# Both score maps of differential attention on the two row halves of TensorE, the minimum written to SBUF, five banks in turn

## The chip, the core and the metric

The kernel runs on one core of a Trainium2 chip. The metric is the device time of one execution in microseconds (us). A lower time is better. Engines are named as in the profile: PE (TensorE matmuls), PEld (TensorE weight loads), DVE (VectorE), ACT (ScalarE), POOL (GpSimd) and SP (SyncE, which issues the DMAs).

## What is computed

Two layers of a decoder trunk over 1024 tokens of width 1024 in float32. Layer 0 has stick-breaking and forgetting heads, layer 1 has 8 differential heads, and each layer ends in a SwiGLU block. The change touches layer 1 alone:

```python
def differential_attention(q1, q2, k1, k2, v, lam, rel_bias):
    ...
    def block(start, end):                       # 128 queries over the causal prefix
        bias = table[t5_bucket(...)].transpose(2, 0, 1)[None]
        s1 = jnp.einsum('bhqd,bhkd->bhqk', q1[:, :, start:end], k1[:, :, :end]) * scale + bias
        s2 = jnp.einsum('bhqd,bhkd->bhqk', q2[:, :, start:end], k2[:, :, :end]) * scale + bias
        p1 = jax.nn.softmax(jnp.where(causal, s1, -jnp.inf), axis=-1)
        p2 = jax.nn.softmax(jnp.where(causal, s2, -jnp.inf), axis=-1)
        return jnp.einsum('bhqk,bhkd->bhqd', p1 - lam * p2, v[:, :, :end])
```

`q1`, `q2`, `k1`, `k2` have 64 channels each, and `v` has 128. The bias differs from a constant only within the nearest 256 keys.

## The kernel before

**Numbers.** Matmuls take float32r operands. A float32 value x is split into h (x rounded to float32r) and l = x - h, and a product is made of the three terms hh, hl and lh. So a dense projection issues three matmuls of 512 columns for each 128-channel step (`mm3`, lines 375 to 377); the value projection issues three of 256 columns (lines 466 to 468).

**Layer 1's mixer.** `mixer(1, ...)` runs eight windows, one for a head. A window (`window_odd`) makes the score rows of its head in two groups g of four 128-query rows (`g_rows`, `row_C`), mixed with the value products of the group before (`g_pv`: the weight rows are transposed by PE at line 677, split, and multiplied with V at line 691). Between these steps `paced` feeds pieces of the "filler": the projections of later heads and, at the end, most of the output projection. Each step yields its estimated PE time, and the filler is advanced in proportion to the yields' sum over a fixed window cost (18000). The build then orders the instructions of each engine by what is ready by its own estimate, so the order on PE is not that of the code.

**Scores of a row.** One projection gives both maps of a head: channels 0 to 63 of the partitions belong to map 1, channels 64 to 127 to map 2. `stack_k` and `stack_q` copy, by DMAs on SP's queue, h and l of one map on top of each other (64 + 64 partitions), so that one matmul over all 128 rows of the array gives two of the four possible terms. `scores` (line 569) then issues two matmuls for each piece of a row and each map, all four terms. A row of n = 128(i+1) keys is cut into pieces of at most 512 columns (`cuts`): over the eight rows of a head that is five pieces of 512, three of 384 and four of 256 columns. So a head has 12 pieces x 2 maps x 2 = 48 score matmuls, and the layer has 384.

**Softmax of a row.** `map_C` adds the bias to the scores in their PSUM bank, in place, and takes the running minimum (of the negated, scaled values) with `tensor_tensor_reduce` on DVE (line 623); then ACT takes the exponential out of PSUM, piece by piece (line 110), with a sum for each piece, and DVE adds the two sums of a row with two pieces (line 630). `row_C` joins the maps: two reciprocals, a product with -lambda (lines 642 to 644), a scaling of map 2 on POOL (line 645) and a multiply-add on DVE (line 646).

**Banks.** PSUM has eight banks: `rD` (two) serves projections, `rS` (three) scores, `rT` (two) transposes and norms, `rO` (one) the value product. Each set is used in turn.

Of the kernel before, what the change touches and what calls it, by code (L numbers as in the profile page):

```python
# [14 lines left out]
AF = mybir.ActivationFunctionType  # L15
# [3 lines left out]
P = 128  # L19
# [3 lines left out]
TH = 512  # L23
# [17 lines left out]
def r32(ap):  # L41
    return ap.bitcast(F32R)
# [74 lines left out]
class Trunk:  # L117
# [277 lines left out]
    def stack_k(self, src, th, KK):  # L395
# [9 lines left out]
            dma(KK[e][o, sl], t[p, 512:1024])  # L405
        self.sr.put(t)

    def head_norm(self, x, gcol, table):

        nc = self.nc  # L410
        sq, h, l = self.hf.get(), self.hr.get(), self.hr.get()
        self.S.activation(r32(h[:]), x[:], AF.Square)
        self.S.activation(sq[:], x[:], AF.Square)
        nc.vector.tensor_tensor(r32(l[:]), sq[:], h[:], ALU.subtract)
        ms = self.rT.get()
        nc.tensor.matmul(ms[:], r32(self.blk[:]), r32(h[:]), start=True, stop=False)
        nc.tensor.matmul(ms[:], r32(self.blk[:]), r32(l[:]), start=False, stop=True)
        self.hr.put(h, l)
        self.rstd(ms[:], sq[:], table)
        nc.vector.scalar_tensor_tensor(x[:], x[:], self.gains[:, gcol:gcol + 1], sq[:], ALU.mult, ALU.mult)  # L420
        self.hf.put(sq)

    def qk_half(self, which, th, w, stk, gcol, table=False, ps=None):

        ps = self.rD.get() if ps is None else ps
        self.dense_half(w[2], w[3], th, ps[:])
        src = self.hf.get()
        self.nc.vector.tensor_tensor(src[:], ps[:], self.rt[:, th * TH:th * TH + TH], ALU.mult)
        if gcol is not None:
            self.head_norm(src, gcol, table)  # L430
        if which == 0:
            if th == 0:
                stk.append([self.sr.get(), self.sr.get()])
            self.stack_k(src, th, stk[0])
        else:
            stk.append([self.sr.get(), self.sr.get()])
            self.pq = gcol is not None
            self.stack_q(src, stk[-1])
        self.hf.put(src)
        self.w_ahead(self.keep)  # L440

    def g_qk(self, st, gains=(None, None), table=False):

        stk = []
        for which in range(2):
            w = self.w_next()
            for th in range(2):
                self.qk_half(which, th, w, stk, gains[which], table)
                if th == 1:
                    self.sr.put(w[0], w[1])  # L450
                    if which == 1:
                        st.append(list(zip(*stk)))
                yield HALF

    def v_weights(self, forget):
# [42 lines left out]
    def first_project(self, st, vs, gains, accs, load, table):  # L498

        w, vh, vl = self.v_weights(False)  # L500
        wq = [self.w_next(), self.w_next()]
        V = [self.sf.get(), self.sf.get()]
        stk = []
        for th in range(2):
            load(th)
            for k in range(KC):
                for t in range(4):
                    self.v_piece(4 * th + t, k, vh, vl, self.bank[t], 256)
            self.rms(accs[th], th, True, table)
# [8 lines left out]
        st.append(list(zip(*stk)))  # L518

    def log_forget(self):  # L520

# [33 lines left out]
    def row_of(self, rows, i):  # L555
        s, o = self.ROWPOS[i]
        return rows[s][:, o:o + (i + 1) * P]

    def scores(self, i, KK, *Q):

        nc = self.nc
        n = (i + 1) * P
        cuts = [(0, max(n, 256))] if n <= 512 else ([(0, 384), (384, 640)] if n == 640 else [(0, 512), (512, n)])
        res = []
        for lo, hi in cuts:
# [44 lines left out]
    def map_C(self, i, stk, w, nb, st):  # L610

        nc = self.nc
        n = (i + 1) * P
        pcs = self.scores(i, *stk)
        near = max(n - 256, 0)
        parts = [(b, lo, min(hi, near), self.zero[:].to_broadcast([P, min(hi, near) - lo])) for b, lo, hi in pcs
                 if min(hi, near) > lo]
        b, lo, hi = pcs[-1]
        parts.append((b, lo, n, nb[:, 256 - (n - near):256]))
        m = self.pinit[:]  # L620
        for j, (b, lo, hi, add) in enumerate(parts):
            d = b[:, max(near - lo, 0) if j == len(parts) - 1 else 0:hi - lo]
            nc.vector.tensor_tensor_reduce(out=d, in0=d, in1=add, scale=-0.125, scalar=m, op0=ALU.add, op1=ALU.min,
                                           accum_out=st[:, j:j + 1])
            m = st[:, j:j + 1]
        for j, (b, lo, hi) in enumerate(pcs):
            self.S.activation(w[:, lo:hi], b[:, 0:hi - lo], AF.Exp, bias=m, scale=-1.0,
                                 accum_out=st[:, 5 + j:6 + j])
        if len(pcs) == 2:
            nc.vector.tensor_tensor(st[:, 7:8], st[:, 5:6], st[:, 6:7], ALU.add)  # L630
            return st[:, 7:8]
        return st[:, 5:6]

    def row_C(self, i, stk, rows, nb):
        nc = self.nc
        n = (i + 1) * P
        w = self.row_of(rows, i)
        p2 = self.sf.get()
        s1, s2, s3 = self.stat.get(), self.stat.get(), self.stat.get()
# [7 lines left out]
        self.sf.put(p2)  # L647

    def g_rows(self, kind, g, stk, rows, extra):
        for i in range(4 * g, 4 * g + 4):  # L650
            if kind == "A":
                self.row_A(i, stk, rows)
            elif kind == "B":
                self.row_B(i, stk, rows, *extra)
            else:
                self.row_C(i, stk, rows, *extra)
            yield max((i + 1) * P, 256) * 2 * (2 if kind == "C" else 1) / 2.4

    def g_pv(self, kind, g, rows, vv, split, done):

# [145 lines left out]
    def mixer(self, l, gains, window, window_cost, accs, load, forget=None):  # L806
# [3 lines left out]
        if l == 0:  # L810
            self.setup2()
        rows = [self.sf.get() for _ in range(4)] + [self.raw.get()]
        dense = self.filler(l, st, vs, gains, forget)
        self.dcost = 0.0
        self.o_done = 0
        V = None
        for w in range(8):
# [7 lines left out]
            att = window(w, stks, V, rows)  # L825
            self.paced(self.last(att, rows) if w == 7 else att, window_cost, dense, lo, hi)
        self.advance(dense, math.inf)

    def filler(self, l, st, vs, gains, forget):
        yield from self.project(st, vs, gains, forget)  # L830
# [40 lines left out]
    def window_odd(self, h, stks, V, rows):  # L871
# [5 lines left out]
        vv = []  # L877
        split = partial(self.split_v128, V, h % 2)
        for g in range(2):
            yield from self.stage(self.g_rows("C", g, stks, rows, (nb,)))  # L880
            fin = None
            self.sr.put(*(x[1 + g] for x in stks))
            if g == 1:
                self.sr.put(*(x[0] for x in stks))
# [8 lines left out]
    def stage(self, rows):  # L893

        pv = self.pend
        if pv is None:
            yield from rows
            return
        yield from self.mix(rows, 4, pv[0], pv[1])
        if pv[2]:  # L900
            pv[2]()

# [512 lines left out]
    def build(self):  # L1415
        nc, b = self.nc, self.bank
        self.pend = None
        self.rD, self.rS, self.rT, self.rO = Rot(b[0:2]), Rot(b[2:5]), Rot(b[5:7]), Rot(b[7:8])
        self.rF, self.rE = Rot(b[0:4]), Rot(b)
        self.make_weights()  # L1420
# [132 lines left out]
```

## Time and profile before

| | |
|---|---|
| median of three runs | 2577.13 us (2576.64 to 2579.63) |
| the profiled execution | 2576.64 us, of which 2574.9 us are its span |
| mean granted TensorE clock | 0.988 |
| busy share of the span | PE 95%, PEld 78%, DVE 76%, ACT 51%, POOL 30% |
| layer 1's mixer, first projection to first gate matmul | 1320 to 1919 us of the span |

A matmul's duration in the trace includes its way through the array, so consecutive matmuls overlap: the time one costs in a stream is the step from its start to the next one's start. "Idle before" is the time an engine had nothing running, and the name behind the arrow is what ended it. "issue" means that nothing the profile shows was waited for.

### The profile page before, as it was taken

The numbers are of one execution on the slowest core, as the hardware profiler recorded it, in microseconds if no ns is written. First come the engines' busy times: TensorE is split into PE (matmuls) and PEld (weight loads), VectorE is DVE, ScalarE is ACT, GpSimd is POOL, SyncE is SP. The second block draws the span as 40 slices with busy tenths as digits, with TensorE's granted clock in tenths as the row PEclk, the third lists the DMA queues.
The fourth block names the chain that finished last, engine by engine and source line by source line (L and its number), as shares of the span: only waits on it lengthen the run. The fifth ranks groups of instructions, "written<-read, shape, count | busy, mean of one in ns | idle before, by whom it ended". The sixth has DMA issues, their size and how long they took to land.

```text
span 2574.9 us, 34805 instructions
## 1 busy us (share of the span) xinstructions
PE 2456.4 (95%) x11896; PEld 2016.9 (78%) x11896; DVE 1946.7 (76%) x3391; ACT 1303.1 (51%) x2618; POOL 764.3 (30%) x608
## 2 busy tenths in 40 slices
PE   8898899999989999999999999998998999999999
PEld 7786778777768888888878878876777788888887
DVE  7969958987987666698576687778879866667974
ACT  5646666764732322344466576766555233234352
POOL 4112111120343322165142232223333333222910
PEclk9999999999989999999999999999999999999999
DMA  6323132465224232474333241325531422318352
GB/s 184 88 54 83 37 97 82 114 185 175 107 100 149 93 120 95 160 249 147 111 125 84 72 101 56 97 79 133 179 126 66 169 99 94 119 66 300 119 185 80
DMA packets 148270, 307.50 MB, mean 119 GB/s; under 512 B 18515, under 2 KB 24436, under 8 KB 148092
## 3 DMA queue, kind: packets, MB, share of 16 engines
q1 hardware_dynamic: 148092, 305.28, 38.0%
q8 instruction: 93, 1.52, 0.2%
q14 instruction: 85, 0.70, 0.1%
HBM read 187.74 MB, written 75.53 MB: 102 GB/s over the span
## 4 chain that ended last, share of the span: by engine, by line
PE 67%; DVE 19%; ACT 6%; issue 4%; DMA 2%; POOL 2%; SPq 0%; DVEq 0%; ACTq 0%; POOLq 0%
PE bk L1129 9%; PE bk L1130 9%; PE bk L1131 9%; PE bk L1278 5%; PE bk L1279 5%; PE bk L1280 5%; PE bk L376 4%; PE bk L375 4%; PE bk L377 4%; PE bk L691 4%; PE bk L569 3%; DVE sf L587 3%; PE bk L677 2%; DVE sr L1062 2%; ACT sf L110 2%
## 5 line engine op out<-in xcount | busy, mean ns | idle before, releaser
L102 ACT CAST sr<-sf 128x512 fp32r<-128x512 f32 (+2 forms) x536 | 337.0, 648 | 572.3 <-PE bk L1131 235.3
L1062 DVE TENSOR_TENSOR sr<-sf,sr 128x512 fp32r<-128x512 f32 x438 | 400.5, 923 | 143.9 <-ACT sr L102 142.6
L1129 PE MATMUL bk<-sr,sr 128*128 128x512 f32 x1232 | 484.3, 393 | 22.1 <-DVE hf L1153 13.3
L1131 PE MATMUL bk<-sr,sr 128*128 128x512 f32 x1232 | 482.2, 392 | 3.4 <-DVE sr L1062 3.4
L1130 PE MATMUL bk<-sr,sr 128*128 128x512 f32 x1232 | 483.0, 392 | 0.0
L375 PE MATMUL bk<-sr,sr 128*128 128x512 f32 x768 | 307.1, 400 | 6.3 <-DVE sf L989 3.5
L376 PE MATMUL bk<-sr,sr 128*128 128x512 f32 x768 | 305.5, 398 | 2.3 <-DVE sr L932 2.2
L377 PE MATMUL bk<-sr,sr 128*128 128x512 f32 x768 | 304.3, 396 | 0.0
L1129 PEld LDWEIGHTS bk<-sr,sr 128*128 128x128 f32 x1232 | 233.7, 190 | 74.1 <-DVE hf L1153 13.6
L221 POOL TENSOR_TENSOR sr<-raw,sr 128x512 fp32r<-128x512 f32 (+2 forms) x140 | 188.1, 1360 | 304.9 <-ACT sr L102 168.1
L1131 PEld LDWEIGHTS bk<-sr,sr 128*128 128x128 f32 x1232 | 233.5, 190 | 53.5 <-DVE sr L1062 4.2
L1130 PEld LDWEIGHTS bk<-sr,sr 128*128 128x128 f32 x1232 | 233.7, 190 | 47.9
L1279 PE MATMUL bk<-sr,sr 128*128 128x512 f32 x616 | 239.9, 389 | 1.4 <-DVE sr L1062 1.4
L1280 PE MATMUL bk<-sr,sr 128*128 128x512 f32 x616 | 239.6, 389 | 0.0
L1278 PE MATMUL bk<-sr,sr 128*128 128x512 f32 x616 | 239.6, 389 | 0.0
L102 ACT CAST sr<-hf 128x512 fp32r<-128x512 f32 (+1 forms) x248 | 153.8, 620 | 112.4 <-DMA hf<-td 43.5
L1062 DVE TENSOR_TENSOR sr<-hf,sr 128x512 fp32r<-128x512 f32 x178 | 180.2, 1016 | 35.7 <-ACT sr L102 34.9
L569 PE MATMUL bk<-sr,sr 128*128 128x512 f32 (+2 forms) x768 | 200.3, 359 | 7.1 <-ACT sf L110 6.3
L691 PE MATMUL bk<-hr,sr 128*128 128x512 f32 (+2 forms) x560 | 165.4, 388 | 13.9 <-DVE hr L709 11.2
L102 ACT CAST hr<-bk 128x512 fp32r<-128x512 f32 (+2 forms) x240 | 122.5, 525 | 102.8 <-PE bk L677 90.5
L375 PEld LDWEIGHTS bk<-sr,sr 128*128 128x128 f32 x768 | 145.3, 189 | 36.8 <-DVE sf L989 5.2
L709 DVE TENSOR_TENSOR hr<-bk,hr 128x512 fp32r<-128x512 f32 (+2 forms) x240 | 142.2, 603 | 39.3 <-ACT hr L102 37.5
(203 smaller groups left out, 4836.8 us busy)
## 6 DMA issues: line engine op xcount, KB each, us to landing
hf<-td SPq DMA_DIRECT2D x146, 256.0 KB, 3.1
td<-hf SPq DMA_DIRECT2D x138, 256.0 KB, 2.0
sr<-sr SPq DMA_DIRECT2D x96, 256.0 KB, 3.4
sf<-in_wg_dram SPq DMA_DIRECT2D x44, 512.0 KB, 3.3
sf<-in_wu_dram SPq DMA_DIRECT2D x44, 512.0 KB, 3.3
sf<-in_wd_dram SPq DMA_DIRECT2D x88, 256.0 KB, 4.9
raw<-in_w_dram SPq DMA_DIRECT2D x64, 256.0 KB, 2.9
sr<-sr SPq DMA_DIRECT2D x128, 128.0 KB, 2.3
```

Source lines behind the costliest of these rows:

```text
L102: self.last = self.e.copy(out, in_)
L375: nc.tensor.matmul(ps, WH[k], hH[k], start=first and k == 0, stop=False)
L376: nc.tensor.matmul(ps, WH[k], hL[k], start=False, stop=False)
L377: nc.tensor.matmul(ps, WL[k], hH[k], start=False, stop=last and k == n - 1)
L569: nc.tensor.matmul(b[:, 0:hi - lo], r32(Q[i // 4][:, q]), r32(KK[:, lo:hi]), start=j == 0, stop=j == 1)
L1062: self.nc.vector.tensor_tensor(r32(t[:, TH:2 * TH]), x, t[:, 0:TH], ALU.subtract)
L1129: nc.tensor.matmul(ps, wh, bh, start=i in (0, 2, 4, 6) and j == 0, stop=False, skip_group_check=True)
L1130: nc.tensor.matmul(ps, wh, bl, start=False, stop=False, skip_group_check=True)
L1131: last = nc.tensor.matmul(ps, wl, bh, start=False, stop=j == 3, skip_group_check=True)
L1278: nc.tensor.matmul(ps, wh, bh, start=i in (0, 6, 2, 4) and j == 0, stop=False, skip_group_check=True)
L1279: nc.tensor.matmul(ps, wh, bl, start=False, stop=False, skip_group_check=True)
L1280: nc.tensor.matmul(ps, wl, bh, start=False, stop=j == self.PAIRS - 1, skip_group_check=True)
```

## The change

For layer 1 (`tiled`), K and Q are no longer stacked. `two_k` and `two_q` write h and l directly, with both maps still in their own 64 partitions; the 7 DMAs of each token half are gone, 112 rows of SP's queue in all. `row_C` makes both maps of a row together: for each piece it takes two banks and issues the terms hh, hl, lh for map 1 on partitions 0 to 63 and for map 2 on partitions 64 to 127, alternating. So each matmul uses half of the array's rows, and there are six for a piece in place of four: 576 in the layer. The minimum writes its result to the row's place in SBUF, so a bank is free once DVE has read it; one exponential then covers the whole row of a map in SBUF, one reciprocal covers both sums, and POOL multiplies by both scalars at once. Scores and transposes share one set of five banks. Each piece is a step of its own for the mixing and pacing, and the window cost is 15000.

```diff
+    def two_q(self, src):
+        t = self.sr.get()
+        self.S.copy(r32(t[:, 0:512]), src[:])
+        self.nc.gpsimd.tensor_tensor(r32(t[:, 512:1024]), src[:], t[:, 0:512], ALU.subtract)
+        return t
+
+    def two_k(self, src, th, h, l):
+        sl = slice(th * TH, th * TH + TH)
+        self.S.copy(r32(h[:, sl]), src[:])
+        self.nc.vector.tensor_tensor(r32(l[:, sl]), src[:], h[:, sl], ALU.subtract)
...
     def row_C(self, i, stk, rows, nb):
...
-        l1 = self.map_C(i, stk[0], w, nb, s1)
-        l2 = self.map_C(i, stk[1], p2, nb, s2)
-        nc.vector.reciprocal(s3[:, 0:1], l1)
-        nc.vector.reciprocal(s3[:, 1:2], l2)
-        nc.vector.tensor_tensor(s3[:, 2:3], s3[:, 1:2], self.neglam[:], ALU.mult)
-        nc.gpsimd.tensor_scalar(p2[:, 0:n], p2[:, 0:n], s3[:, 2:3], 0.0, ALU.mult, ALU.add)
-        nc.vector.scalar_tensor_tensor(w, w, s3[:, 0:1], p2[:, 0:n], ALU.mult, ALU.add)
+        half = [slice(0, 64), slice(64, 128)]
+        for lo, hi in self.cuts(n):
+            if lo > 0:
+                yield (lo * 3) / 2.4
+            banks = [self.rS.get(), self.rS.get()]
+            for x, (a, c) in enumerate(((qh, kh), (qh, kl), (ql, kh))):
+                for e in range(2):
+                    nc.tensor.matmul(banks[e][:, 0:hi - lo], r32(q[half[e], a]), r32(c[half[e], lo:hi]),
+                                     start=x == 0, stop=x == 2)
...
+                    nc.vector.tensor_tensor_reduce(out=(w, p2)[e][:, a:c], in0=banks[e][:, a - lo:c - lo], in1=add,
+                                                   scale=-0.125, scalar=m[e], op0=ALU.add, op1=ALU.min,
+                                                   accum_out=mins[e][:, j:j + 1])
...
+        for e in range(2):
+            x = (w, p2)[e][:, 0:n]
+            self.S.activation(x, x, AF.Exp, bias=m[e], scale=-1.0, accum_out=st[:, e:e + 1])
+        nc.vector.reciprocal(st[:, 2:4], st[:, 0:2])
+        nc.gpsimd.tensor_scalar(p2[:, 0:n], p2[:, 0:n], st[:, 3:4], self.neglam[:], ALU.mult, ALU.mult)
+        nc.vector.scalar_tensor_tensor(w, w, st[:, 2:3], p2[:, 0:n], ALU.mult, ALU.add)
...
+        if self.tiled:
+            self.rS = self.rT = Rot(self.bank[2:7])
...
-        self.mixer(1, lambda i: (G_DK, G_DQ), self.window_odd, 18000.0, self.acc, lambda th: None)
+        self.mixer(1, lambda i: (G_DK, G_DQ), self.window_odd, 15000.0, self.acc, lambda th: None)
```

In the lists of order below, line 569 is the score matmul of before and line 653 that of the changed kernel; `bk_65` to `bk_69` are five PSUM banks. PE before, a row of 512 keys in an early window (head 1): each map is one bank with two matmuls, both over the whole array.

```order
L691 MATMUL bk_70<-hr_12709,sr_12186 128x512
L569 MATMUL bk_65<-sr_12052,sr_12270 128x512 x2
L416 MATMUL bk_68<-hr_12759,blk 128x512
L569 MATMUL bk_66<-sr_12053,sr_12271 128x512 x2
L375 MATMUL bk_64<-sr_11230,sr_12440 128x512
```

PE after, a row of 512 keys in one of the next windows: `sr_12709` holds h of K and `sr_12710` l; the two banks, and with them the two row halves, alternate.

```order
L377 MATMUL bk_64<-sr_11237,sr_12911 128x512
L653 MATMUL bk_67<-sr_12709,sr_12907 128x512
L653 MATMUL bk_68<-sr_12709,sr_12907 128x512
L653 MATMUL bk_67<-sr_12710,sr_12907 128x512
L653 MATMUL bk_68<-sr_12710,sr_12907 128x512
L653 MATMUL bk_67<-sr_12709,sr_12907 128x512
L653 MATMUL bk_68<-sr_12709,sr_12907 128x512
L703 MATMUL bk_69<-ident,sf_11977 128x128
```

Three neighbouring pairs stand between two matmuls over the whole array. PE before, the first pieces of the row of 640 keys in that early window:

```order
L691 MATMUL bk_70<-z,sr_12186 128x256
L569 MATMUL bk_67<-sr_12052,sr_12391 128x384 x2
L569 MATMUL bk_65<-sr_12052,sr_12391 128x256 x2
L569 MATMUL bk_66<-sr_12053,sr_12392 128x384 x2
L375 MATMUL bk_63<-sr_11230,sr_12450 128x512
```

PE after, the row of 640 keys in the same window as above (703 is the transpose, 717 the value product):

```order
L489 MATMUL bk_63<-sr_13126,sr_11240 128x256
L653 MATMUL bk_67<-sr_12709,sr_12998 128x384
L653 MATMUL bk_67<-sr_12710,sr_12998 128x384
L653 MATMUL bk_67<-sr_12709,sr_12998 128x384
L703 MATMUL bk_68<-ident,sf_11978 128x128
L653 MATMUL bk_66<-sr_12709,sr_12998 128x384
L717 MATMUL bk_70<-z,sr_12843 128x256 x2
L717 MATMUL bk_70<-z,sr_12844 128x256
L653 MATMUL bk_66<-sr_12710,sr_12998 128x384
L653 MATMUL bk_66<-sr_12709,sr_12998 128x384
L703 MATMUL bk_68<-ident,sf_11979 128x128
```

Here the build has pulled the two maps apart: each bank's three matmuls follow each other, with work over the whole array between them.

## Rows read from the trace of the kernel before

**Rows 1.** The page, part 1: busy us, share of the span, instructions.

```profile
PE 2456.4 (95%) x11896; PEld 2016.9 (78%) x11896; DVE 1946.7 (76%) x3391; ACT 1303.1 (51%) x2618; POOL 764.3 (30%) x608
```

**Rows 2.** Busy time by stretch: length, engines, granted clock, DMA share, GB/s.

```profile
1320.00:1919.00 599.00, 564.98 (x2980) 460.78 (x2979) 435.62 (x1162) 375.83 (x874) 182.37 (x159) 0.99 0.37 104
1780.00:1820.00 40.00, 31.85 (x134) 23.93 (x135) 32.36 (x83) 21.02 (x52) 15.35 (x14) 0.87 0.63 182
```

**Rows 3.** Groups of PE, 1320 to 1919 us: busy us, mean ns | idle before, releasers.

```profile
L375 PE MATMUL bk<-sr,sr 128*128 128x512 f32 x380 | 151.0, 398 | 4.4 <-ACT sr L102 2.6 <-DVE sf L989 1.7
...
L569 PE MATMUL bk<-sr,sr 128*128 128x512 f32 (+2 forms) x384 | 99.4, 359 | 6.0 <-ACT sf L110 5.8
```

**Rows 4.** PE in order of time, 1500 to 1506 us: start, us, what [idle before].

```profile
1500.03 0.40 PE L375 MATMUL bk<-sr,sr 128*128 128x512 f32 x1
1500.26 0.40 PE L417 MATMUL bk<-hr,blk 128*128 128x512 f32 x1
...
1502.40 0.60 PE L677 MATMUL bk<-ident,sf 128*128 128x128 f32 x4
```

**Rows 5.** PE and PEld in order of time, 322.5 to 324.4 us, around L545.

```profile
322.66 0.28 PE L467 MATMUL bk<-sr,sr 128*128 128x264 f32 x1
...
322.78 0.28 PE L468 MATMUL bk<-sr,sr 128*128 128x264 f32 x1
...
322.99 0.39 PE L545 MATMUL bk<-hf,nb 128*8 128x128 f32 x2
...
323.31 0.19 PEld L375 LDWEIGHTS bk<-sr,sr 128*128 128x128 f32 x1 [0.22 <-issue]
323.31 0.50 PE L375 MATMUL bk<-sr,sr 128*128 128x512 f32 x1
...
323.41 0.19 PEld L376 LDWEIGHTS bk<-sr,sr 128*128 128x128 f32 x1
323.64 0.39 PE L376 MATMUL bk<-sr,sr 128*128 128x512 f32 x1
...
323.87 0.40 PE L377 MATMUL bk<-sr,sr 128*128 128x512 f32 x1
```

**Rows 6.** PE and PEld in order of time, 8 to 11 us, around L296.

```profile
8.78 1.00 PE L296 MATMUL bk<-sr 33*128 33x384 f32 x2
9.72 0.50 PEld L466 LDWEIGHTS bk<-sr,sr 128*128 128x128 f32 x2 [0.44 <-issue]
9.72 0.79 PE L466 MATMUL bk<-sr,sr 128*128 128x256 f32 x2
...
10.31 1.05 PE L467 MATMUL bk<-sr,sr 128*128 128x256 f32 x4
```

**Rows 7.** Waits of PE and PEld, 1376 to 1876 us: us in total, times, longest.

```profile
PE bk L677 <- DVE sf L646: 4.5, 6, 1.5
PE bk L691 <- DVE z L703: 3.4, 2, 2.7
...
PEld bk L569 <- ACT sf L110: 15.6, 36, 1.4
```

**Rows 8.** Groups of DVE and ACT by shape: busy us, mean ns | idle before.

```profile
L623 DVE DVE_READ_ACCUMULATOR2_ANT st<- 128x1 f32 x256 | 36.1, 141 | 0.0
L603 DVE DVE_READ_ACCUMULATOR2_ANT st<- 128x1 f32 x96 | 7.8, 82 | 0.0
L630 DVE TENSOR_TENSOR st<-st 128x1 f32<-128x1 f32 x64 | 21.0, 328 | 11.4 <-ACT sf L110 11.3
L644 DVE TENSOR_TENSOR st<-st,neglam 128x1 f32<-128x1 f32 x64 | 12.4, 194 | 1.1
L110 ACT ACTIVATE sf<-bk,st 128x512 f32<-128x512 f32 x72 | 49.5, 691 | 32.1 <-DVE st L623 18.1 <-DVE st L642 11.1 <-DVE st L644 2.7
L110 ACT ACTIVATION_READ_ACCUMULATOR sf<-bk,st 128x1 f32 x184 | 37.8, 205 | 0.0
L110 ACT ACTIVATE sf<-sf,st 128x1024 f32<-128x1024 f32 x8 | 9.2, 1151 | 1.9 <-DVE st L603 1.8
```

More of the change, by code (lines that the diff above doesn't have):

```diff
@@ L430, in qk_half @@
             self.head_norm(src, gcol, table)
-        if which == 0:
+        if self.tiled:
+            if which == 0:
+                if th == 0:
+                    stk += [self.sr.get(), self.sr.get()]
+                self.two_k(src, th, *stk[0:2])
+            else:
+                stk.append(self.two_q(src))
+        elif which == 0:
             if th == 0:
@@ L451, in g_qk @@
                     if which == 1:
-                        st.append(list(zip(*stk)))
+                        st.append(stk if self.tiled else list(zip(*stk)))
                 yield HALF
@@ L517, in first_project @@
         vs.append(V)
-        st.append(list(zip(*stk)))
+        st.append(stk if self.tiled else list(zip(*stk)))
     def log_forget(self):
@@ L557, in row_of, with cuts @@
         return rows[s][:, o:o + (i + 1) * P]
+    @staticmethod
+    def cuts(n):
+        return [(0, max(n, 256))] if n <= 512 else ([(0, 384), (384, 640)] if n == 640 else [(0, 512), (512, n)])
     def scores(self, i, KK, *Q):
@@ L608, in row_B @@
         nc.vector.tensor_scalar(w, w, st[:, 6:7], 0.0, ALU.mult, ALU.add)
[L610 to L632, printed above, removed]
     def row_C(self, i, stk, rows, nb):
@@ L646, in row_C @@
-        nc.vector.scalar_tensor_tensor(w, w, s3[:, 0:1], p2[:, 0:n], ALU.mult, ALU.add)
+        kh, kl, q = stk[0], stk[1], stk[2 + i // 4]
+        w, p2 = self.row_of(rows, i), self.sf.get()
+        near = max(n - 256, 0)
+        st, mins = self.stat.get(), [self.stat.get(), self.stat.get()]
+        m = [self.pinit[:]] * 2
+        j = 0
+        qh, ql = (slice(c * TH + (i % 4) * P, c * TH + (i % 4) * P + P) for c in range(2))
+        half = [slice(0, 64), slice(64, 128)]
+        for lo, hi in self.cuts(n):
+            if lo > 0:
[5 more added lines that the diff above has]
+                                     start=x == 0, stop=x == 2)
+            end = min(hi, n)
+            parts = [(a, c) for a, c in ((lo, min(end, near)), (max(lo, near), end)) if c > a]
+            for a, c in parts:
+                add = nb[:, 256 - (n - a):256 - (n - c)] if a >= near else self.zero[:].to_broadcast([P, c - a])
+                for e in range(2):
+                    nc.vector.tensor_tensor_reduce(out=(w, p2)[e][:, a:c], in0=banks[e][:, a - lo:c - lo], in1=add,
+                                                   scale=-0.125, scalar=m[e], op0=ALU.add, op1=ALU.min,
+                                                   accum_out=mins[e][:, j:j + 1])
+                    m[e] = mins[e][:, j:j + 1]
+                j += 1
@@ L647, in row_C @@
+        for e in range(2):
+            x = (w, p2)[e][:, 0:n]
[3 more added lines that the diff above has]
+        nc.vector.scalar_tensor_tensor(w, w, st[:, 2:3], p2[:, 0:n], ALU.mult, ALU.add)
         self.sf.put(p2)
+        yield (max(n, 256) - lo) * 3 / 2.4
     def g_rows(self, kind, g, stk, rows, extra):
@@ L655, in g_rows @@
             else:
-                self.row_C(i, stk, rows, *extra)
-            yield max((i + 1) * P, 256) * 2 * (2 if kind == "C" else 1) / 2.4
+                yield from self.row_C(i, stk, rows, *extra)
+                continue
+            yield max((i + 1) * P, 256) * 2 / 2.4
     def g_pv(self, kind, g, rows, vv, split, done):
@@ L879, in window_odd @@
         for g in range(2):
-            yield from self.stage(self.g_rows("C", g, stks, rows, (nb,)))
+            yield from self.stage(self.g_rows("C", g, stks, rows, (nb,)), 4 * g + 4)
             fin = None
-            self.sr.put(*(x[1 + g] for x in stks))
+            self.sr.put(stks[2 + g])
             if g == 1:
-                self.sr.put(*(x[0] for x in stks))
+                self.sr.put(*stks[0:2])
                 def fin():
@@ L891, in window_odd, with stage @@
             self.pend = (self.g_pv("C", g, rows, vv, split, self.o_sub(1, h, g)), 4 * g + 5, fin)
-    def stage(self, rows):
+    def stage(self, rows, steps=4):
         pv = self.pend
@@ L898, in stage @@
             return
-        yield from self.mix(rows, 4, pv[0], pv[1])
+        yield from self.mix(rows, steps, pv[0], pv[1])
         if pv[2]:
```

10 lines of the change are left out of this document (5 added, 5 removed).

## The prediction, made before the changed kernel was run

> **What bounds the kernel now.** I read the page's busy shares first. PE is busy for 95% of the span and its weight loads for 78%, with no other engine above 76% [rows 1]. So a step that PE gains or loses moves the end, unless PE waits for something else there. The built order of the changed kernel is that of before up to layer 1's mixer, and the gate and down projections behind it issue the same matmuls. Everything has to come from the stretch 1320 to 1919 us. There PE shows work for 565 of 599 us, DVE for 436, ACT for 376 [rows 2]. So 34 us are idle at most, and the 565 contain the way of each matmul through the array, which hides part of the stalls. One slice stands out: from 1780 to 1820 us PE works 32 of 40 us and its granted clock falls to 0.87, so below the 2.4 GHz level for a part of it, after waiting [rows 2].
>
> A matmul costs its step, not its duration. The 384 score matmuls last 359 ns in the mean [rows 3], but in a stream 512 columns step by 0.23 us (1500.03 to 1500.26) [rows 4] and 264 columns by 0.12 us (322.66 to 322.78) [rows 5]. For 384 columns I take 0.18, between them. Four transposes of 128 columns take 0.60 us against 0.27 to 0.28 us for one, a step of 0.11 us [rows 4]; each has a weight load of its own and few columns, so I read this as the pace of 128-column loads.
>
> **The change on PE: the score matmuls.** Over 8 heads the pieces are 40 of 512, 24 of 384 and 32 of 256 columns. Before, each has four matmuls: 160 x 0.23 + 96 x 0.18 + 128 x 0.12 = 69.5 us. After, each has six. If halves of the array take turns, this is 1.5 times as much, 104.2 us (+34.7). If a matmul on the lower rows and its neighbour on the upper rows run side by side, each pair costs one step, and six would cost three. But the order gives pairs only in part: of 576 matmuls 194 neighbouring pairs use different halves and banks (101 of them with 512 columns, 46 with 384, 47 with 256), and 188 stand without a partner (50, 47 and 91), since the build often gives one bank its three matmuls in a row. Pairs side by side: 101 x 0.23 + 46 x 0.18 + 47 x 0.12 = 37.1 us; single ones 11.5 + 8.5 + 10.9 = 30.9 us; together 68.0 us, 1.5 us less than before. If the two loads of a pair go one after the other at 0.11 us, no pair is below 0.22 us, and the shorter ones add 46 x 0.04 + 47 x 0.10 = 6.5 us: +5.0. No row of before shows two halves at work at once, so the bounds are -1.5 and +34.7. I take **+2**: the two matmuls of a pair share no array row, no operand partition and no bank, and what they could share, the path of the loads, has a price in the transposes' row that adds only 6.5 us.
>
> The Trainium skill bears on both ends. "TensorEngine Tiling (Array Packing)", section Tiling Modes, says that different tiles can load weights and multiply in parallel; by this the term would be -1.5, and no run here shows it yet. "TensorE: Matmul & The Clock Gate", part 3, says that a load overlaps a running matmul only where the row groups differ. By that the 188 single matmuls would each show their load, 188 x 0.11 = 21 us more; but the trace has L376's load starting at 323.41 us while L375, over the same rows, still runs, and done before the next start [rows 5]. The measurement decides, and nothing is added.
>
> **The change on PE: its shape.** All work around the scores uses the whole array. The order has 128 groups of half-array matmuls, so 128 entries and 128 exits. Before has no such switch in layer 1, but two places elsewhere show one. At 322.99 us a matmul with 8 weight columns follows L468: it starts 0.21 us after it, where the step is 0.12, so 0.09 late. Then L375 over the whole array: its load starts at 323.31 only, PEld idle for 0.22 us by "issue", and the matmul behind it comes at 323.64, 0.33 later, where the step is 0.23 [rows 5]. Two L545 take 0.11 a step by their 0.39 us for two against 0.28 for one of that size, so L375's load should have been due at 323.21. An exit costs 0.10 of empty array plus 0.10 of a load that nothing hides: **0.20 us**. The same is seen for rows, though slower, at the start: L296 uses 33 rows, and L466 behind it at 9.72 us has its load after 0.44 us of "issue", and takes 0.59 us for two matmuls where the four of L467 step by about 0.21 us, 0.17 more [rows 6]. An entry should cost the same: 0.09 of empty array and the load of 128 columns, 0.11, shown. So 256 x 0.20 = 51 us. Some of it is not new: 113 of the 256 matmuls at a boundary carry a wait, and a wait that comes late shows the load anyway. Before, the scores' loads waited 36 times for ACT among 384 matmuls [rows 7, 3]; if some 45 of the 113 do, 45 x 0.11 = 5 us were paid already. I take **+46**. The bounds are +51 and, if a switch between half and whole rows were free where L545 and L296 were not, 0.
>
> **What is relieved.** (a) The banks. The scores' loads wait 15.6 us for ACT's exponential, which holds the bank [rows 7]. After, DVE's minimum releases it and five banks turn. Not all goes, since DVE is the next to be waited for: -12 of 15.6. (b) DVE. The read of the minimum takes 141 ns in L623 and 82 in L603, which writes to SBUF as the changed one does: 256 x 59 = 15 us. The additions L630 go, 21.0 us and 11.4 us in which DVE stood for ACT; the products L644 go, 12.4 us [rows 8]; and 64 of the 128 reciprocals at about 0.16 us, 10 us. That makes 58 us of work. (c) ACT. A row of 1024 takes 1151 ns out of SBUF in one piece, where two pieces of 512 take 2 x 691 and one more accumulator read of 205 ns: 0.44 us for each of 64 long rows, 28 us [rows 8]. (d) 112 DMAs leave SP's queue. Of (b) to (d) most is worth nothing, because PE sets the pace: it pays where PE waits for DVE, as for L646 and L703, 7.9 us together [rows 7], and in the clock of the slice at 1780 us, 40 x 0.13 = 5 us. I take -8 of these 13. Together **-20**, with bounds of 0 and the 34 us that PE is idle at all.
>
> New waits: a score matmul now queues behind DVE's list, and a bank shared with transposes can be held by either; everything behind it on PE stands. Of this I have only the 5.8 us of idle time that L569 has behind ACT [rows 3]; the same again is inside the range.
>
> **Sum.** +2 + 46 - 20 = +28 us on 2576.64, so 2604.6; the median lies 0.5 us over the profiled run, which gives **2605**. The bounds of the last two terms make its own range 2587 to 2625.
>
> **Rivals.**
> 1. *The switch is cheap* (faster). It decides below (20 - 2) / 256 = 0.07 us for each boundary. For it: L545 is narrower in columns, and L296 stands at the very start where PE runs at half pace; neither is a 64-row matmul in a warm stream. Against it: both show the same two parts. At 0 to 0.05 us the sum is 2 + (0 to 13) - 20: 2559 to 2572. Chance 0.27.
> 2. *The halves take turns*: the change doesn't do what its words say. The loads and streams of a pair then go one after the other. For it: no row shows two matmuls at once. Against it: they share nothing but PE's queue. +35 + 46 - 20 = +61: 2638, from 2626 to 2652. Chance 0.18.
> 3. *The switch is half hidden*, because PE was about to wait there anyway: 0.07 to 0.11 us for each boundary, 2577 to 2587 with the same relief; a little of this is no change. Chance 0.10.
>
> **How the numbers follow.** The forecast has 0.45. A measurement of this kernel tells 0.2%, about 5 us, from no change. Slower by more: 0.45 + 0.18 + half of rival 3 = 0.67, less 0.02 for the low tail of the forecast, 0.65. Same: 0.07. Faster: 0.28. Faster and slower cases both matter here, so the range reaches from the low end of rival 1 to the middle of rival 2: 2558 to 2642 leaves out about 0.1 on either side; the forecast's own range stands above.
>
> **What would show it.** In the changed trace the starts of neighbouring score matmuls on different halves should lie about 0.11 us or less apart for 512 columns, with 0.23 for each pair; if they lie 0.23 apart, rival 2 holds. At the first score matmul of a group and the first one behind it, PEld should be idle by "issue" for some 0.2 us; if loads run ahead there, rival 1 holds. The mixer's stretch should grow from 599 to about 627 us, with all the difference in it. L569's wait for ACT should be gone, DVE's busy time lower by about 58 us and ACT's by about 28. I am wrong if PE's idle time falls by much more than 20 us, or if PE now waits for DVE at the banks.

## The result and the profile after

The changed kernel takes **2606.33 us** (median of 4 runs, 2602.61 to 2608.94) against 2576.89 us for the kernel before: a ratio of 1.0114, with a 95% interval of 1.0101 to 1.0127. It is slower by 29 us. The profiled execution took 2605.35 us with a span of 2603.6 us, 28.7 us longer than the span of before. The first line below is the page's busy shares; then come two stretches (length, then busy us of PE, PEld, DVE, ACT and POOL, granted clock, DMA share, GB/s); they answer to [rows 1, 2].

```profile
PE 2496.2 (96%) x12088; PEld 2020.0 (78%) x12088; DVE 1915.9 (74%) x3199; ACT 1292.8 (50%) x2490; POOL 773.9 (30%) x608
```

```profile
1320.00:1949.00 629.00, 601.99 (x3169) 460.38 (x3170) 407.19 (x969) 364.50 (x746) 187.20 (x159) 0.99 0.20 66
1780.00:1820.00 40.00, 38.17 (x163) 26.81 (x161) 32.12 (x68) 26.91 (x53) 10.72 (x9) 0.87 0.28 91
```

The mixer of layer 1 grew from 599 to 629 us, and that is the whole difference. PE shows 37 us more work in it and DVE 28 us less. The slice from 1780 to 1820 us has the same low granted clock as before, 0.87, though PE now shows work for 38 of its 40 us. But it is low in another place: from 1800 us on (0.77 and 0.72 in the two stretches of 10 us), where before it was low up to 1800 (0.88 and 0.61).

Next, PE and PEld in order of time around one group of 512 columns (start, us, what, idle before), and then PE around one of 256 columns. L653 is the new score matmul, six in a group.

```profile
1466.73 0.39 PE L376 MATMUL bk<-sr,sr 128*128 128x512 f32 x1
1466.95 0.39 PE L377 MATMUL bk<-sr,sr 128*128 128x512 f32 x1
1467.27 0.53 PEld L653 LDWEIGHTS bk<-sr,sr 64*128 64x128 f32 x6 [0.35 <-issue]
1467.27 0.96 PE L653 MATMUL bk<-sr,sr 64*128 64x512 f32 x6
1468.16 0.14 PEld L703 LDWEIGHTS bk<-ident,sf 128*128 128x128 f32 x1 [0.37 <-issue]
1468.17 0.33 PE L703 MATMUL bk<-ident,sf 128*128 128x128 f32 x1
```

```profile
1428.60 0.28 PE L489 MATMUL bk<-sr,sr 128*128 128x256 f32 x1
1428.81 0.62 PE L653 MATMUL bk<-sr,sr 64*128 64x256 f32 x6
1429.36 0.33 PE L703 MATMUL bk<-ident,sf 128*128 128x128 f32 x1
```

Six matmuls of 512 columns are done in 0.90 us (1467.27 to 1468.17), where six steps of 0.23 would be 1.38 and three are 0.69: the two halves do run side by side. The other 0.21 us, and the 0.09 by which the group starts late (0.32 after L377, where the step is 0.23), are the two changes of shape. At either end PEld stands for about 0.35 us by "issue": no load runs ahead over the boundary. This holds throughout: at all 128 entries and all 128 exits the load starts within 3 ns of its matmul, whereas in the stream of before L376's load starts 0.22 us ahead of it. In the second group the entry is late by the same 0.09 us (0.21 against 0.12) and the rest takes 0.55 us instead of 3 x 0.12.

Last, groups of PE, DVE and ACT from 1320 to 1949 us (busy us, mean ns, idle before) and the waits of PEld from 1376 to 1905 us (us in total, times, longest). They answer to [rows 3, 7, 8].

```profile
L653 PE MATMUL bk<-sr,sr 64*128 64x512 f32 (+2 forms) x576 | 103.9, 385 | 1.3 <-DVE st L660 1.0 <-ACT hf L110 0.2
...
L660 DVE DVE_READ_ACCUMULATOR2_ANT st<- 128x1 f32 x256 | 21.1, 82 | 0.0
...
L668 DVE RECIPROCAL st<-st 128x2 f32<-128x2 f32 x64 | 10.4, 162 | 20.7 <-ACT sf L110 20.2 <-ACT raw L110 0.3
...
L427 DVE TENSOR_TENSOR hr<-hf,hr 128x512 fp32r<-128x512 f32 x32 | 26.4, 826 | 10.0 <-ACT hf L110 8.6 <-ACT hr L110 0.7
...
L110 ACT ACTIVATE sf<-sf,st 128x1024 f32<-128x1024 f32 x16 | 18.3, 1144 | 0.1
```

```profile
PEld bk L653 <- issue: 19.2, 68, 0.4
PEld bk L429 <- ACT hr L110: 12.0, 25, 1.4
PEld bk L703 <- issue: 7.0, 25, 0.4
PEld bk L703 <- DVE sf L670: 5.6, 8, 1.7
...
PEld bk L653 <- DVE st L660: 4.9, 13, 0.7
```

The scores' wait for ACT, 15.6 us before [rows 7], has become 4.9 us for DVE's minimum. In its place stand 19.2 us by "issue" ahead of the scores and 7.0 us ahead of the transposes behind them.

### The profile page after: what moved, and what is told of

Its sections match the earlier page's. It is cut to its first block, busy times and chain, and to the rows that moved or that the text cites. A ratio compares the mean times of both kernels' runs of the same rounds, so it can differ in the third digit from the quotient of the medians.

```text
span 2603.6 us, 34533 instructions
## 1 busy us (share of the span) xinstructions
PE 2496.2 (96%) x12088; PEld 2020.0 (78%) x12088; DVE 1915.9 (74%) x3199; ACT 1292.8 (50%) x2490; POOL 773.9 (30%) x608
## 4 chain that ended last, share of the span: by engine, by line
PE 69%; DVE 16%; ACT 5%; issue 5%; POOL 3%; DMA 2%; SPq 0%; DVEq 0%; ACTq 0%; POOLq 0%
PE bk L1159 9%; PE bk L1161 9%; PE bk L1160 9%; PE bk L1310 5%; PE bk L1308 5%; PE bk L1309 5%; PE bk L375 4%; PE bk L376 4%; PE bk L377 4%; PE bk L717 4%; DVE sf L612 3%; PE bk L703 2%; DVE sr L1092 2%; PE bk L653 2%; ACT sf L110 2%
## 5 line engine op out<-in xcount | busy, mean ns | idle before, releaser
L376 PE MATMUL bk<-sr,sr 128*128 128x512 f32 x768 | 306.7, 400 | 0.4 <-DVE sr L962 0.3
L377 PE MATMUL bk<-sr,sr 128*128 128x512 f32 x768 | 304.9, 397 | 0.0
L1159 PEld LDWEIGHTS bk<-sr,sr 128*128 128x128 f32 x1232 | 233.9, 190 | 71.6 <-DVE hf L1183 11.2
L221 POOL TENSOR_TENSOR sr<-raw,sr 128x512 fp32r<-128x512 f32 (+2 forms) x140 | 194.8, 1407 | 288.4 <-ACT sr L102 149.5
L1161 PEld LDWEIGHTS bk<-sr,sr 128*128 128x128 f32 x1232 | 233.6, 190 | 53.5 <-DVE sr L1092 4.2
L1160 PEld LDWEIGHTS bk<-sr,sr 128*128 128x128 f32 x1232 | 233.9, 190 | 48.2
L375 PEld LDWEIGHTS bk<-sr,sr 128*128 128x128 f32 x768 | 145.7, 190 | 38.7 <-DVE sf L1019 5.1
L377 PEld LDWEIGHTS bk<-sr,sr 128*128 128x128 f32 x768 | 145.7, 190 | 29.5 <-issue 0.4
```

Source lines behind the costliest of these rows:

```text
L375: nc.tensor.matmul(ps, WH[k], hH[k], start=first and k == 0, stop=False)
L376: nc.tensor.matmul(ps, WH[k], hL[k], start=False, stop=False)
L377: nc.tensor.matmul(ps, WL[k], hH[k], start=False, stop=last and k == n - 1)
L1159: nc.tensor.matmul(ps, wh, bh, start=i in (0, 2, 4, 6) and j == 0, stop=False, skip_group_check=True)
L1160: nc.tensor.matmul(ps, wh, bl, start=False, stop=False, skip_group_check=True)
L1161: last = nc.tensor.matmul(ps, wl, bh, start=False, stop=j == 3, skip_group_check=True)
```

## The experiments

All times are medians, and each ratio is against the kernel before, measured beside it. Beside the time there is a second measure, an account of layer 1's mixer from its first value-projection matmul to its first gate matmul. From the start of each PE matmul to the start of the next I take off the step that its size has in an undisturbed stream of the same trace: 0.228 us for 512 columns, 0.177 for 384, 0.119 for 256, 0.108 for a transpose that another follows and 0.027 for the last one. What is left is put down "at the scores" when a score matmul stands at one of its two ends or just before it, and "elsewhere" otherwise. A pair on two halves counts as one step; I take two half-array matmuls for a pair when they start less than about half a step apart. Where that line is drawn matters: if only starts within 0.06 us count, the changed kernel has 67.8 us of score steps and 61.3 on top, with the same sum. The steps of all other work come to 450 us in every kernel of the table. The table has one profiled execution of each kernel. The start of the mixer, up to which all kernels issue the same on PE, lies anywhere from 1318.7 to 1323.9 us in these executions and those of e3, e4 and e12, so differences of a few us between two executions mean little.

| kernel | mixer, us | score steps | on top, at the scores | on top, elsewhere |
|---|---|---|---|---|
| before | 598.8 | 68.7 | 27.8 | 51.9 |
| after | 629.0 | 65.4 | 63.8 | 49.9 |
| e1, stacked scores | 590.2 | 68.7 | 20.7 | 50.4 |
| e2, and banks three and two | 587.9 | 68.7 | 19.4 | 49.5 |
| e5, one half's three first | 631.6 | 70.2 | 62.0 | 48.9 |
| e6, six whole-array matmuls | 619.5 | 103.1 | 16.8 | 49.6 |
| e10, after with three and two | 626.5 | 66.6 | 58.4 | 52.2 |

The 63.8 us of the changed kernel divide into 18.8 at the entries, 16.0 within the groups (the first load that nothing hides), 19.5 at the exits and 9.5 at the load after that.

**e1: the change without its half-array matmuls.** The softmax, the minimum to SBUF and the five banks are those of the changed kernel; the scores are the four whole-array products of before on stacked operands. With them come back the DMAs that stack and the window cost of 18000.

```diff
-            for x, (a, c) in enumerate(((qh, kh), (qh, kl), (ql, kh))):
-                for e in range(2):
-                    nc.tensor.matmul(banks[e][:, 0:hi - lo], r32(q[half[e], a]), r32(c[half[e], lo:hi]),
-                                     start=x == 0, stop=x == 2)
+            for e in range(2):
+                for x in range(2):
+                    nc.tensor.matmul(banks[e][:, 0:hi - lo], r32(stk[e][1 + i // 4][:, qs[x]]),
+                                     r32(stk[e][0][:, lo:hi]), start=x == 0, stop=x == 1)
```

> The changed kernel with the scores of before: K and Q stacked, two matmuls over the whole array for each map and piece, window cost 18000; kept are the minimum to SBUF, one exponential per row, the joint reciprocal, POOL's double product and the five banks in turn. Theory (the loss is the change of array shape, 256 times about 0.19 us, against a relief of some 18 us and no gain in the streams): 18 us under before, 2559, from 2554 to 2565. Rival A (the relief is nothing, and the shape costs only the 30 us that were lost): 2577, as before. Rival B (the new softmax order itself costs time and the half-array matmuls are innocent): 2590 or more.

Measured: 2570.41 us, ratio 0.997 (0.996 to 0.9979). This is between the theory (2559) and rival A (2577): without the half-array matmuls the kernel beats that of before, so what they brought with them is what makes the changed kernel slow, but the relief is 7 us and not 18. The score loads still wait for DVE's minimum, in a few long waits (1376 to 1930 us, as for e2 below):

```profile
PEld bk L644 <- DVE st L651: 5.9, 8, 2.0
```

**e2: the same, with the banks divided as before**, three for the scores and two for the rest, instead of five in turn for both.

```diff
-            self.rS = self.rT = Rot(self.bank[2:7])
+            pass
```

> As the run with stacked scores and five banks, but with the banks of before, three for scores and two for transposes and norms. The prediction gave the banks 12 of 20 us of relief, in which early release and five banks are not told apart. If the early release (DVE reads, ACT no longer) is what counts: within 4 us of the run with five banks, 2557 to 2565. If the five banks count: 2567 to 2573. If they harm (transposes and scores block each other): below the run with five banks.

Measured: 2564.28 us, 0.9954 (0.9939 to 0.9969). The five banks in turn, which I had counted as a gain, cost about 6 us beside e1 by the medians. In the mixer of the profiled executions, the only part in which the two kernels differ, it is 2.3 us (590.2 and 587.9), so the size stays open between 2 and 6. The longest wait of a score load for DVE falls from 2.0 to 1.1 us:

```profile
PEld bk L644 <- DVE st L651: 4.8, 10, 1.1
```

**e3 and e4: the price of a change of shape by itself.** The kernel before, with one more matmul of 64 columns ahead of each piece of the first map's scores (96 in all); its result is overwritten by the matmul behind it. In e3 it uses 64 rows, so that the array changes shape twice; in e4 it uses all 128 rows.

```diff
+                nc.tensor.matmul(b[:, 0:64], r32(Q[i // 4][0:64, (i % 4) * P:(i % 4) * P + P]),
+                                 r32(KK[0:64, lo:lo + 64]), start=True, stop=True)
```

> The kernel before with one more matmul of 64 columns on 64 rows ahead of each piece of map 1, 96 in all, into the bank that the piece then overwrites; nothing else is changed and nothing is left out. Each stands alone between whole-array matmuls, so 96 entries and 96 exits. Theory: 192 x 0.19 plus 96 x 0.03 to 0.11 for the matmul, 39 to 47 us: 2616 to 2624, less what falls on waits, so 2608 at least. Rival (a switch is mostly hidden in waits, or costs under 0.07 us): 2580 to 2593.

> The control to the run with 64 rows: the same 96 matmuls of 64 columns over all 128 rows, so no change of shape. Both theories: 96 x 0.03 to 0.11 us, 3 to 11 us: 2580 to 2588. The difference of the two runs is the price of 192 changes of shape: 30 to 37 us by the theory, 10 at most by its rival.

Measured: e3 2602.56 us, 1.0105 (1.0088 to 1.0122), between its two ranges; e4 2589.22 us, 1.0051 (1.0036 to 1.0066), a little above its range. PE in order of time around one of the added matmuls (L568; the scores behind it are L572), first in e3 and then at the same place of e4:

```profile
1444.07 0.28 PE L468 MATMUL bk<-sr,sr 128*128 128x256 f32 x1
1444.28 0.29 PE L568 MATMUL bk<-sr,sr 64*128 64x64 f32 x1
1444.50 0.74 PE L572 MATMUL bk<-sr,sr 128*128 128x256 f32 x4
1445.08 0.60 PE L682 MATMUL bk<-ident,sf 128*128 128x128 f32 x4
```

```profile
1445.95 0.28 PE L468 MATMUL bk<-sr,sr 128*128 128x256 f32 x1
1446.07 0.20 PE L568 MATMUL bk<-sr,sr 128*128 128x64 f32 x1
1446.10 0.71 PE L572 MATMUL bk<-sr,sr 128*128 128x256 f32 x4
1446.66 0.60 PE L682 MATMUL bk<-ident,sf 128*128 128x128 f32 x4
```

From L468 to L682 e3 takes 1.01 us and e4 0.71, so the two changes of shape cost 0.30 us here, 0.15 each. The entry is 0.09 late (0.21 where the step is 0.12), and the scores start 0.22 us behind the added matmul instead of 0.03: empty array and a load that nothing hides. The next load shows in both runs, 0.10 us at the step behind it in e3 and 0.08 in e4, since a matmul of 64 columns is too short to cover it; so the difference leaves out most of that one. By the medians of all 96 places the difference is again 0.30 us, 29 us in all, close to the 30 to 37 that I expected.

But the times differ by 13.3 us only, and the mixers of the profiled executions by 11.4 (623.4 and 612.0), 0.06 to 0.07 for each of 192 changes. The rest is waits. Without the price of the added matmuls themselves, what lies on top of the steps is 80 us in the kernel before, 82 in e4 and 64 in e3: PE spent in changes of shape time that it would have waited anyway. So in a kernel whose scores still wait for ACT, less than half of the price reaches the time.

**e5: one half's three products first**, then the other's.

```diff
-            for x, (a, c) in enumerate(((qh, kh), (qh, kl), (ql, kh))):
-                for e in range(2):
+            for e in range(2):
+                for x, (a, c) in enumerate(((qh, kh), (qh, kl), (ql, kh))):
```

> The changed kernel with its two loops swapped: the three terms of map 1 first, then the three of map 2. In the built order 81 neighbouring pairs on different halves are left (194 before the swap) and 123 groups (128). By the steps of 0.23, 0.18 and 0.12 us the score streams need 88 us where they needed 67. Theory (pairs run side by side): 21 us more for the streams, 2 less for the groups: 2625, from 2618 to 2632. Rival (the halves take turns in time after all, though their starts lie close): within 4 us of the changed kernel, 2602 to 2610.

Measured: 2610.46 us, 1.0132 (1.0099 to 1.0164). The order has 81 neighbouring pairs instead of 194, yet the scores' steps grow by 5 us only. PE in order of time around one group:

```profile
1531.15 0.39 PE L377 MATMUL bk<-sr,sr 128*128 128x512 f32 x1
...
1531.47 0.97 PE L653 MATMUL bk<-sr,sr 64*128 64x512 f32 x6
...
1532.36 0.33 PE L703 MATMUL bk<-ident,sf 128*128 128x128 f32 x1
```

Six matmuls again take 0.89 us, entered 0.32 us after L377. Their records start at 0, 10, 335, 344, 570 and 580 ns, and the two that release DVE are the fifth and the sixth, though they were issued a a a b b b. So PE starts the second half's matmuls beside the first half's that were issued ahead of them, and my counting of pairs by the order was the wrong count. My theory's range (2618 to 2632) is missed for that reason. The rival's (2602 to 2610) ends where the median lies, but its mechanism is not what happened: six matmuls in turn would take 1.36 us and not 0.89.

**e6: six whole-array matmuls.** The same loops, operands and banks as in the changed kernel, with all 128 rows for each product, so that each map's scores are the sum of both maps.

```diff
-        half = [slice(0, 64), slice(64, 128)]
+        half = [slice(0, 128), slice(0, 128)]
```

> The changed kernel with its six matmuls a piece over all 128 rows: no change of shape and nothing side by side. Each bank then gets the sum of both maps' scores, so this leaves the separation of the maps out. Theory: the streams take 103 us in place of 67 (+36), the 256 switches are gone (-49): 2594, from 2587 to 2601. Rival A (the switches cost only the 30 us that were lost): +36 - 31, 2611. Rival B (the loss lies in the new order or in waits of the softmax, not in the matmuls' shape): 2642.

Measured: 2597.13 us, 1.0073 (1.005 to 1.0095), as expected. Though its score steps are 103.1 us against 65.4, it is 9 us *faster* than the halves side by side:

```profile
1490.28 0.39 PE L377 MATMUL bk<-sr,sr 128*128 128x512 f32 x1
1490.51 1.52 PE L653 MATMUL bk<-sr,sr 128*128 128x512 f32 x6
1491.87 0.27 PE L703 MATMUL bk<-ident,raw 128*128 128x128 f32 x1
```

The entry is one step (0.23 us), and six steps of 0.227 make the 1.36 us to L703, with nothing at the exit. In the account what lies on top at the scores is 16.8 us against 63.8. This is the cleanest pair of the study, since only the rows differ, and the built order on PE is the same, matmul for matmul: 63.8 - 16.8 = 47.0 us for 256 boundaries, 0.18 each. Beside e1 it is 63.8 - 20.7 = 43.1 us, 0.17 each.

**e7, e8, e9, e11: fewer boundaries.** If a boundary costs 0.18 us, fewer and longer groups should win it back. e7 binds the six matmuls of a piece into a critical section, e8 those of a whole row. e9 (a piece) and e11 (a row) bind them by order alone: the group's first matmul behind the PE instructions written before it, and all that are written later behind its last.

```diff
+            with self.tc.tile_critical():
```

```diff
+        for i in before[-24:]:
+            self.after_ins(made[0], i)
+        for x, y in zip(made, made[1:]):
+            self.after_ins(y, x)
```

> The changed kernel with the six matmuls of a piece bound together, so that the build puts nothing between them: 95 groups in place of 128 and all 288 pairs as neighbours. Theory: streams 51.5 in place of 67 us (-15), 66 switches fewer at 0.19 (-13): 2578, from 2572 to 2590, since six matmuls that may not be parted wait for two free banks at once. Rival (waits for the second bank eat it): 2600 or more.

> The changed kernel with all matmuls of a row bound together, both pieces of a long row, four banks of the five at once: 64 groups and 288 pairs. Theory: streams -15, 128 switches fewer at 0.19 (-24): 2567 if nothing waits, 2567 to 2585 with the wait for four banks. Rival (the wait for four banks of five decides): 2595 or more, with PE waiting for DVE's minimum in the trace.

> The changed kernel with the six matmuls of a piece kept together by order alone, with no added wait: 84 groups in place of 128, all but five pairs as neighbours. Theory (a switch costs some 0.16 us as the run with six whole-array matmuls showed, and halves work side by side): 88 switches fewer (-14), streams 51.5 in place of 65 us (-14): 2578, from 2572 to 2590. Rival (keeping them together makes PE wait for the second bank or hold back other work): 2600 or more, with PE's idle time before the group's first matmul in the trace.

> As the run with pieces kept together by order alone, but for both pieces of a long row: 62 groups, 288 pairs, four of five banks at once. Theory without waits: 132 switches fewer (-21) and -14 for the streams: 2571. Rival (four banks at once make PE wait for DVE's minimum): 2590 or more. Which side wins tells whether groups can be merged at all with five banks.

Measured: 2706.04 us (1.0503, 1.0476 to 1.053), 2674.46 (1.0373, 1.035 to 1.0396), 2727.0 (1.0594, 1.0575 to 1.0613) and 2728.49 (1.0592, 1.0578 to 1.0607). All four miss by some 90 us and more, and say nothing of the boundaries. The critical section puts semaphore waits and a drain on PE's own queue ahead of the groups (96 drains with a median of 0.76 us at L651 in e7), for which DVE waits, and PE's loads stand by "issue" ahead of each of the 95 groups (e7, waits from 1376 to 1980 us):

```profile
DVE sf L661 <- PEq L651: 137.9, 71, 5.3
PEld bk L654 <- issue: 119.8, 95, 4.7
```

With the order alone PE takes no other ready work while it waits for the norms (L429, L430 and L812). e9's waits of PE, 1376 to 2010 us, and its mixer:

```profile
PE bk L429 <- ACT hr L110: 30.7, 24, 3.1
...
PE bk L430 <- DVE hr L427: 23.4, 27, 1.6
...
PE bk L812 <- DVE hr L809: 19.6, 12, 3.3
```

```profile
1320.00:2068.00 748.00, 629.82 (x3177) 481.78 (x3176) 410.90 (x972) 372.35 (x748) 183.70 (x159) 0.90 0.17 55
```

PE is idle for 118 of these 748 us, and its granted clock is 0.90 instead of 0.99, below the 2.4 GHz level for a part of it. In the account the stalls elsewhere are 145.5 us (e9) and 184.5 (e11) instead of 49.9. e11 has 62 groups instead of 128 and about as much on top at its scores (61 us) as the changed kernel, but with stalls of this size that doesn't isolate the boundary. Whether a schedule with long groups and without these stalls would beat the kernel before stays open.

**e10: the changed kernel with three and two banks**, by e2's edit.

> The changed kernel with the banks of before, three for scores and two for transposes and norms; 123 groups and 190 pairs in the built order. With stacked scores the three and two banks were 6 us better than five in turn. If that holds here too: 2600, from 2596 to 2604. Rival: a piece takes two banks, so three give no second piece ahead, and PE waits for DVE: 2612 or more.

Measured: 2602.44 us, 1.0099 (1.0085 to 1.0113), 4 us under the changed kernel's median, as in e2 though smaller. Their intervals overlap, so this pair alone would not show it.

**e12: e2's kernel once more**, to settle whether it beats both.

> The run with stacked scores, SBUF minimum, one exponential per row and the banks of before once more, with more rounds, since it was the fastest: 2564, a ratio of 0.9954 to the kernel before, if the first measurement holds; within 0.2% of before if it was chance.

Measured: 2565.39 us, 0.9956 (0.9943 to 0.9968), after 0.9954 in e2. Its mixer is 589.3 us. The version with the new softmax, the old stacked scores and the old banks is some 11 us faster than the kernel before and 41 us faster than the changed one.

## Why the prediction came out

**The place was right.** The mixer grew by 30.2 us (598.8 to 629.0) and the whole span by 28.7.

**The score stream (+2): the halves side by side were right, the price of the loads was not.** Steps went from 68.7 to 65.4 us, -3.3 (-0.9 by the stricter count of pairs). The two matmuls of a pair start 3 ns apart, and three pairs of 512 start at 0, 335 and 570 ns; pairs of 256 columns follow each other by 0.12 us, so the two 128-column loads of a pair go in at once and not one after the other at 0.11 as I had allowed for. The Trainium skill, "TensorEngine Tiling (Array Packing)", section Tiling Modes, has different tiles load and multiply in parallel; the trace agrees, with the 3 ns and the 0.12 us above. My lower bound of -1.5 counted pairs by the order of issue; e5 shows that PE makes pairs of matmuls that are not neighbours, so it was no bound.

**The change of shape (+46): right.** 43 us beside e1 and 47 beside e6, 0.17 to 0.18 us for each of 256 boundaries. The reading of L545 [rows 5], one matmul in another stage and with another cut of the array, gave 0.20 less what was already paid. Both of its parts stand in the new trace: 0.09 us of empty array at the entry, and a load of about 0.1 us that nothing hides, with PEld idle by "issue" ahead of it 68 times. The Trainium skill, "TensorEngine Tiling (Array Packing)", section Tiling Modes, says that changing the mode drains the array; the trace agrees, with the 0.09 us by which the entries are late, here and in e3.

**The relief (-20): the step that failed.** It came to about -9: 27.8 to 20.7 at the scores (e1), 7.1 us, and 51.9 to 50.4 elsewhere, 1.5 us. There were three errors. The 15.6 us that I started from are a wait of the load engine, part of which passes while a matmul still runs; PE itself was idle for 6.0 us ahead of L569 [rows 3], close to the 7.1 that came. I took -12 for the banks "since DVE is the next to be waited for", and put the five banks in turn on the side of the gain. By e2 they belong on the other side: the wait for ACT went, but with three banks of its own for the scores the kernel is 6 us faster by the medians and 2.3 by the mixers (e1, e2), or 4 and 2.5 with overlapping intervals (after, e10). That a rotation shared with transposes makes a score wait for whatever held the next bank in turn is my reading of the shorter longest wait in e2; it is argued, not shown. And I took -8 for DVE, ACT and the clock. DVE's small operations shrank just as their rows said: the reads 36.1 to 21.1 us, L630 and L644 gone, one reciprocal of two columns for two, together the 58 us forecast. But DVE's busy time fell by 31 us only (1946.7 to 1915.9), since the records of short instructions overlap their neighbours' (in the mixer the sum of DVE's records fell by 53 us, 514.9 to 462.2) and others grew (L427 takes 826 ns, the same subtraction 711 as L414 before). The clock of the slice at 1780 us stayed at 0.87. From 1802 to 1806 us, before the clock falls, PE waits 0.40, 0.61 and 0.60 us for operands of the norms (L784, L430, L785), which the change doesn't touch. What the DMAs that left SP's queue and the window cost of 15000 brought has no run of its own.

**The sum** is -3.3 + 43.1 - 8.6 = +31 us by the account, with 30.2 in the mixer and 29.4 by the medians, against +28 forecast. So the good figure owes something to luck, in two errors of opposite sign: 5 us too much for the stream and 11 too much relief. My own bounds took the relief to be 0 to 34, and the measured value lies inside. The forecast's own range was not worked out well: with the relief at 34 and the rest as forecast the sum is 2591, not 2587, and the bound of 0 for the shape's term isn't in it at all. The chances of a slower kernel add up to 0.68, not 0.67.

**The rivals.** The cheap switch needed under 0.07 us per boundary; 0.17 and the load that starts only with its matmul at every boundary exclude it. Halves that take turns would show 0.23 us between partners; they show 0.003. The half-hidden switch needed 0.07 to 0.11. It holds for the kernel of before: of 0.15 by the steps of e3 and e4 some 0.07 reached the time. In the changed kernel, whose scores no longer wait for ACT, it doesn't: beside e6 all of 0.18 is left.

**What would have shown it.** Starts, entry, the mixer's length, L569's wait and the rows of DVE's small operations came as written. The pace of pairs was right (0.235 us) except for the first of a group, 0.335, which carries the exposed load. DVE's busy time, -31 instead of -58, and ACT's, -10 (1303.1 to 1292.8) instead of -28, did not; ACT's records, too, fell by more in their sum (446.3 to 414.5 in the mixer) than in their union. PE's idle time in the mixer fell by 7 us, from 34 to 27. And one sign of being wrong came in part: the score loads now wait 4.9 us for DVE at the banks, PE itself 1.0.

## What to carry to other kernels

Three pairs on two row halves take three steps where the stacked form takes four, a saving of 0.12 to 0.23 us for a piece, but entry and exit together cost about 0.35 us; so by this sum a group has to hold two or three pieces before it pays, and it must be one that PE can run without waiting. No run here shows such a group paying. Before packing, look for any matmul in the trace that uses part of the array and read the gap on either side of it: that one row carried the largest term here. And a price at single instructions is not yet one in the time: in e3 more than half of it fell on waits that stood there anyway. Last, try the parts of a change apart: this change held an improvement of 11 us (one exponential per row, the minimum to SBUF) under a loss of some 40 (43 at the boundaries of the halves, 3 back in the streams) and one of 2 to 6 (the shared banks).

## What was not expected of the hardware

- PE does not keep the order of issue between the two halves. Three matmuls on the one half, issued behind three on the other, start beside them (0, 10, 335, 344, 570, 580 ns in e5), and six take 0.89 us like the six of the alternating kernel (0.90).
- Six whole-array matmuls of 512 columns end in 1.36 us and six half-array ones in 0.90, yet by the medians the kernel with the former is 9 us faster (2597.13 against 2606.33): the changes of shape cost more than the streams save.
- Binding matmuls together was dear here: 68 to 122 us over the changed kernel, with critical sections by drains and waits on PE's queue (e7), with order alone by waits of PE for other engines' results (e9).
